# Two seams of an up projection in a decoder step: operands in a written order, sums moved between engines

## The chip, the cores and the metric

The kernel runs on one core of a Trainium2 chip. A core has five engines with queues of their own: TensorE (PE, matmuls; PEld is its weight load), VectorE (DVE), ScalarE (ACT), GpSimd (POOL) and SyncE (SP, which here only issues DMAs). Each works off its instructions in order and waits on semaphores. The metric is the device time of one execution in microseconds, lower is better.

## The reference

One step of a single-layer hybrid decoder for 1024 prompt rows and 64 sample rows of width 1024 (1088 rows, handled here as two halves of 544). What matters here is the end of it:

```python
merged = jax.nn.sigmoid(ga) * (o_a @ w_a_out[i]) + jax.nn.sigmoid(gb) * (o_b @ w_b_out[i])
x = x + merged @ w_o[i]
h2 = rmsnorm(x, g_mlp[i])
x = x + jnp.square(jax.nn.relu(h2 @ w_up[i])) @ w_down[i]
y = rmsnorm(x, g_final).astype(out_dtype)
```

w_o is 1024 x 1024, w_up 1024 x 4096, w_down 4096 x 1024, all in 32-bit floats.

## The kernel before

Every 32-bit product is made of three matmuls: each operand is split into a high part (a cast, on ScalarE) and a low part (operand minus high part, on VectorE; called a low below), and high x high, high x low and low x high are summed in PSUM (`mm3`, `product`). `split` is that pair of instructions; their rows are `z<-..., CAST` and `z<-...,z TENSOR_TENSOR`.

*Output projection.* `project(c)` makes x + merged @ w_o for half c of the rows in eight steps of 128 output features, 48 matmuls each, two halves, so 16 steps; steps 13, 14 and 15 in the text are the last three. A step loads its weights and its part of x, splits the weights (`weights`, wh and wl), and after the matmuls adds x on VectorE (`scalar_tensor_tensor`, L1132, PSUM to `tmp`), stores the sum (x1_d) by a GpSimd DMA, scales it into F on ScalarE (L1137), squares it (L1142), adds the squares on GpSimd (L1143), takes differences in F on VectorE (L1144) and splits seven such blocks into the operands of the up projection (`ops`, kept in `self.B`). `norm2` (L1161) makes 1 / rms of the rows out of the squares: in its first half twelve one-column matmuls (six cuts), then a reciprocal root of ten small VectorE rows (`rsqrt`, L91 to L96); in its second half six transposes and a copy to `rb`.

*Up projection.* It runs with Strassen's scheme in Winograd's form: two k halves, two column halves, seven products for each of 16 pairs of 128 columns. `a_raw` loads the weights of a pair (two `raw`, 512 KB each), `a_op(i, q)` makes operand q of pair i, with sums S on VectorE for q = 2 to 5. `up_pair` runs the seven products in banks b1, b2 and b3 of PSUM: each run q is 24 matmuls for both halves of the rows (12 for pair 0, which is done half by half: c=0, then c=1); between the runs it copies a bank (`copied`, L1245), adds (`plus`, L1264), takes relu and rb (`done`: scalar_tensor_tensor L1251, Square L1252), takes differences on GpSimd (`less`, L1260), and stores the results with DMAs of SyncE (`keep`, F_d). A run that goes on in bank b1 waits for the copy of what is in it.

*Down projection.* It runs in steps over groups of 512 inner rows (g), halves of the rows (c) and of the columns (pp), again with seven products in the order 0, 3, 2, 1, 4, 5, 6 (`down_step`). Its B operands come back from F_d (`db_load`, `db_op`), its A operands from w_down (`da_raw`, sums `da_sum` on GpSimd, `da_op`); `low` makes the low part of either. Results are added to x1: for products 0, 2 and 4 through a copy on ScalarE (L1471) and an add on GpSimd (L1475), for the others by an add on VectorE that reads PSUM.

*What sets the order.* Up to the end of `project` a scheduler of the framework orders the instructions. `up_all` and `down_all` stand in `manual_schedule`: there each engine's order is that of the code. What is made for later steps is put between the runs by `side(q)`, before or after the copies of a run (`before`, `after`), and, from pair 14, by events with a due time (`plan_down`, `events`; the last up run is at about -1, the first down product at 0, two units per run in the up projection). `slot` gives SBUF places by the time until which each is used. The first seam is the passage from output projection to pair 0, the second the passage from pair 15 to the first down step.

## Time and profile before

| | |
|---|---|
| runs | 1541.91, 1543.89, 8198.35 us (median 1543.89) |
| the profiled execution | 1539.15 us, span of its instructions 1536.7 us |
| TensorE busy | 97% of the span, 10,907 matmuls |
| VectorE, ScalarE, GpSimd busy | 72%, 40%, 26% |
| granted TensorE clock, mean | 0.993 of full speed |
| output projection, steps 14 and 15 | TensorE from 804.4 to 816.5 us |
| up projection | 816.5 to 1167.8 us |
| down projection | from 1167.8 us |

The page lists busy time by engine, the span in 40 slices, the chain of work that ended last, the costliest groups of instructions and the DMA issues. The trace behind it answers for a stretch: the instructions of an engine in order of time (start, duration, engine, line, operation, output<-inputs, shapes, count, and in brackets the idle time before with what ended it), who waited for whom, and busy time and granted clock in chosen stretches. In such rows successive alike instructions are merged, and buffer numbers are left out.

### The profile page before, as it was taken

Reading aid. Unit: us, or ns where it says so; the run is one execution under the profiler, and the core shown is the slowest. Engines: PE = TensorE matmul, PEld = TensorE weight load, DVE = VectorE, ACT = ScalarE, POOL = GpSimd, SP = SyncE. Lnnn points to the kernel's source line nnn. Section 1 sums busy time; section 2 is a strip of 40 time slices with the busy share of each in tenths; the row PEclk is TensorE's granted clock in tenths of the full one; section 3 lists DMA queues with packets and bytes.
Section 4 is the critical chain, followed back from the end, with each engine's and each line's share of the span. In section 5 each row is a group of like instructions: output and inputs, shape, how many; then the busy total and the mean of one; then the engine's idle time right before and its main releaser. Section 6 shows DMA issues by size and latency. Waiting matters only on the chain.

```text
span 1536.7 us, 28328 instructions
## 1 busy us (share of the span) xinstructions
PE 1485.0 (97%) x10907; PEld 1446.0 (94%) x10907; DVE 1102.4 (72%) x2192; ACT 609.6 (40%) x1299; POOL 405.2 (26%) x336
## 2 busy tenths in 40 slices
PE   6999999999999999999999999999998999999996
PEld 5889999998998999999998999999997999999996
DVE  8686867757746256555878676666667999999985
ACT  5342332423413224222654443434435445445444
POOL 3200000000001012100332233222345666555641
PEclk9999999999999999999999999999999999999999
DMA  6432331332232434444553443344447544454423
GB/s 219 150 99 53 100 91 49 110 96 73 65 100 68 133 92 131 144 135 123 182 160 128 135 155 132 130 141 155 153 152 264 189 148 126 147 158 137 150 65 117
DMA packets 192367, 198.01 MB, mean 129 GB/s; under 512 B 22036, under 2 KB 157693, under 8 KB 192225
## 3 DMA queue, kind: packets, MB, share of 16 engines
q1 hardware_dynamic: 186953, 183.98, 38.2%
q0 software_dynamic: 4080, 12.13, 2.4%
q8 instruction: 85, 1.39, 0.4%
q14 instruction: 49, 0.40, 0.1%
q10 hardware_dynamic: 1200, 0.10, 0.1%
HBM read 132.10 MB, written 64.19 MB: 128 GB/s over the span
## 4 chain that ended last, share of the span: by engine, by line
PE 86%; DVE 6%; DMA 4%; ACT 2%; issue 1%; SPq 0%; DVEq 0%; ACTq 0%
PE pp L1228 21%; PE pp L1465 21%; PE pm L147 10%; PE pm L148 10%; PE pm L149 10%; PE pt L728 2%; PE pp L147 2%; PE pp L149 2%; PE pp L148 2%; DMA qk<-g_d 2%; PE pt L84 1%; DMA z<-F_d 1%; PE pp L84 1%; DVE r L108 1%; PE pc L817 1%
## 5 line engine op out<-in xcount | busy, mean ns | idle before, releaser
L1228 PE MATMUL pp<-z,z 128*128 128x272 f32 x2688 | 342.0, 290 | 7.5 <-ACT tmp L1245 4.9
L1228 PEld LDWEIGHTS pp<-z,z 128*128 128x128 f32 x2688 | 340.6, 190 | 8.4 <-ACT tmp L1245 5.3
L1465 PE MATMUL pp<-z,z 128*128 128x272 f32 x2688 | 343.0, 289 | 3.6 <-ACT tmp L1471 3.0
L1465 PEld LDWEIGHTS pp<-z,z 128*128 128x128 f32 x2688 | 339.2, 189 | 4.3 <-ACT tmp L1471 3.2
L147 PE MATMUL pm<-hi,wh 128*128 128x384 f32 (+1 forms) x840 | 283.6, 338 | 0.1
L148 PE MATMUL pm<-lo,wh 128*128 128x384 f32 (+1 forms) x840 | 281.6, 335 | 1.3 <-DVE lo L423 1.3
L149 PE MATMUL pm<-hi,wl 128*128 128x384 f32 (+1 forms) x840 | 279.7, 333 | 0.0
L148 PEld LDWEIGHTS pm<-lo,wh 128*128 128x128 f32 x840 | 159.1, 189 | 3.5 <-DVE lo L423 1.8
L147 PEld LDWEIGHTS pm<-hi,wh 128*128 128x128 f32 x840 | 158.9, 189 | 2.5 <-DVE hi L419 0.5
L149 PEld LDWEIGHTS pm<-hi,wl 128*128 128x128 f32 x840 | 159.0, 189 | 0.2
L1475 POOL TENSOR_TENSOR z<-z,tmp 128x544 f32<-128x544 f32 x75 | 110.5, 1473 | 136.6 <-ACT tmp L1471 136.6
L1451 DVE TENSOR_TENSOR z<-z 128x544 fp32r<-128x544 f32 x112 | 136.6, 1231 | 5.0 <-ACT z L1446 5.0
L136 DVE TENSOR_TENSOR wl<-wr,wh 128x1024 fp32r<-128x1024 f32 x57 | 69.8, 1224 | 55.6 <-ACT wh L135 49.0
L135 ACT CAST wh<-wr 128x1024 fp32r<-128x1024 f32 x57 | 59.8, 1049 | 122.5 <-PE pm L148 74.8
L1471 ACT COPY tmp<-pp 128x544 f32<-128x544 f32 x75 | 46.0, 614 | 151.8 <-PE pp L1465 151.8
L1044 DVE TENSOR_TENSOR z<-raw,z 128x512 fp32r<-128x512 f32 x48 | 65.2, 1382 | 36.8 <-ACT z L1043 36.7
L1475 DVE TENSOR_TENSOR z<-z,pp 128x544 f32<-128x544 f32 (+1 forms) x101 | 71.3, 706 | 26.7 <-PE pp L1465 25.1
L1260 POOL TENSOR_TENSOR tmp<-tmp,tq 128x544 f32<-128x544 f32 (+1 forms) x17 | 21.9, 1288 | 238.9 <-ACT tmp L1252 238.9
L1446 ACT CAST z<-z 128x544 fp32r<-128x544 f32 x112 | 70.4, 648 | 12.0 <-DMA z<-F_d 11.9
L149 PE MATMUL pp<-z,wl 128*128 128x272 f32 x256 | 74.1, 289 | 0.0
L147 PE MATMUL pp<-z,wh 128*128 128x272 f32 x256 | 73.9, 289 | 0.0
L148 PE MATMUL pp<-z,wh 128*128 128x272 f32 x256 | 73.6, 288 | 0.0
(344 smaller groups left out, 2510.9 us busy)
## 6 DMA issues: line engine op xcount, KB each, us to landing
z<-F_d SPq DMA_DIRECT2D x112, 272.0 KB
wr<-in_w_in_dram SPq DMA_DIRECT2D x33, 512.0 KB
raw<-in_w_up_dram SPq DMA_DIRECT2D x32, 512.0 KB
raw<-in_w_down_dram SPq DMA_DIRECT2D x32, 512.0 KB
F_d<-tmp SPq DMA_DIRECT2D x60, 272.0 KB
wr<-in_w_o_dram SPq DMA_DIRECT2D x16, 512.0 KB
F_d<-t SPq DMA_DIRECT2D x30, 272.0 KB
tmp<-xT_d SPq DMA_DIRECT2D x16, 272.0 KB
```

The lines of the kernel that those rows point to most:

```text
L135: nc.scalar.copy(out=hi, in_=raw)
L136: (nc.gpsimd if early else nc.vector).tensor_tensor(out=lo, in0=raw, in1=hi.bitcast(F32), op=ALU.subtract)
L147: mm(ps, lhsT=wh, rhs=xh, start=first, stop=False)
L148: mm(ps, lhsT=wh, rhs=xl, start=False, stop=False)
L149: mm(ps, lhsT=wl, rhs=xh, start=False, stop=last)
L1044: (eng or self.nc.vector).tensor_tensor(out=lo, in0=f, in1=hi.bitcast(F32), op=ALU.subtract)
L1228: mm(out, lhsT=l[:, k, :], rhs=r[:, k, :], start=first and k + n == 0, stop=k == 3 and n == 2, skip_group_check=not first)
L1446: self.nc.scalar.copy(out=hi, in_=lo.bitcast(F32))
L1451: self.nc.vector.tensor_tensor(out=lo, in0=f, in1=hi.bitcast(F32), op=ALU.subtract)
L1465: nc.tensor.matmul(ps[:, p, 0:CB], lhsT=l[:, k, p, :], rhs=r[:, k, :], start=first and j + k + n == 0, stop=j == len(gs) - 1 and k == 1 an ...
L1471: nc.scalar.copy(out=t, in_=ps[:, :, 0:CB])
L1475: eng.tensor_tensor(out=x, in0=x, in1=t, op=ALU.add)
```

## The change

1. `project` is taken apart into `fetch`, `parts`, `project`, `x1`, `b_op`; steps 13 to 15 (`project_end`) now stand in the written order. Step 15's addition of x comes inside pair 0's first half (after run 0), and its seven operands are spread over the runs there and one run of the second half. Pair 0's first three operands and its sums S are made behind step 14, the sums in place in `raw`.
2. `norm2` cuts the 544 rows into five pieces instead of six; its second half for c=1 is called at run 6 of pair 0's first half instead of run 5.
3. Operands of pair 1 are made one run later or more, those of pair 2 in the last four runs of pair 1, two at a time. Pairs 1 and 15 put `side` behind the copies of a run; pairs 2 to 14 ahead of them, as before.
4. Sums of the first w_down group (g = 0) on VectorE, at written times from -24 on; loads of the first w_down operand at -28, at the end of pair 13; due times of the first A operands spread. The differences of pair 15 (`less`) on VectorE.
5. The first down step adds all products on VectorE out of PSUM (`direct`), and its `side` comes behind the add.
6. Three more places X, and a smaller scratch for DMA descriptors (`dynamic_dma_scratch_size=4096`).

```diff
+                for n in (13, 14):
+                    self.fetch(n)
+                self.parts(13)
                 with tc.manual_schedule():
+                    self.project_end()
                     self.up_all()
...
+    def project_end(self):
+        for n in (13, 14, 15):
+            self.project(n)
+            if n < 15:
+                self.parts(n + 1)
+            if n == 13:
+                self.fetch(15)
+            elif n == 14:
                 self.a_raw(0)
+            else:
+                self.a_op(0, 0)
+                self.a_op(0, 1)
+                self.a_sum0(0)
+                self.a_op(0, 2)
+            if n < 15:
+                self.after(n)
...
-        cuts = [(b, j, min(P, CB - j * P)) for b in range(2) for j in range(3)]
+        cuts = [(n, n * P, min(P, CT - n * P)) for n in range(5)]
...
-            nc.gpsimd.tensor_tensor(out=at(o), in0=at(a), in1=at(b), op=ALU.subtract)
+            (v if i == 15 else nc.gpsimd).tensor_tensor(out=at(o), in0=at(a), in1=at(b), op=ALU.subtract)
...
         def first(q):
             self.t += 1
             if q == 0:
+                self.a_sum0(1)
                 self.a_raw(1)
-            if q < 3:
-                self.a_op(0, q + 4)
-            if q in (3, 5):
-                self.norm2(1, self.acc1, q == 5)
+            if q < 4:
+                self.a_op(0, q + 3)
+            if q >= 3:
+                b_op((1, 2, 4, 5)[q - 3])
+            if q in (3, 6):
+                self.norm2(1, self.accs[1], q == 6)
         def second(q):
             self.t += 1
             if q == 0:
+                b_op(6)
                 self.a_raw(2)
-            self.a_op(1, q)
+            if q >= 3:
+                self.a_op(1, q - 3)
...
-        self.up_pair(0, (0,), first, True)
-        self.up_pair(0, (1,), second)
+        self.up_pair(0, (0,), lambda q: q or self.x1(15), first)
+        self.up_pair(0, (1,), nothing, second)
+        ops = {(i, q): [(i + 1, q)] for i in range(1, 16) for q in range(7)}
+        ops.update({(1, q): [[(1, 4)], [(1, 5)], [(1, 6)], [(2, 0), (2, 1)], [(2, 2), (2, 3)], [(2, 4), (2, 5)], [(2, 6)]][q]
+                    for q in range(7)})
...
-            self.up_pair(i, (0, 1), side)
+            self.up_pair(i, (0, 1), *((side, nothing) if 1 < i < 15 else (nothing, side)))
...
-                u = 2 * u - 5 if (g, n) == (0, 0) else u
+                z = (-22, -9, -11, -18, -7, -5, -3)[q] if (g, n) == (0, 0) else u - 6
                 if q == 0:
-                    at(u - 20, self.da_raw, g, n)
+                    at(-28 if (g, n) == (0, 0) else u - 20, self.da_raw, g, n)
                 if 2 <= q < 6:
-                    at(max(u - 10, -14), self.da_sum, g, n, q)
+                    j = (3, 2, 4, 5).index(q)
+                    at(u - 10 if g else ((-24, -22, -20, -9), (-6, -4, -2, 5))[n][j], self.da_sum, g, n, q)
...
-        po = self.nc.gpsimd
+        po = self.nc.gpsimd if g else self.nc.vector
...
-                add(x, copied(b), po)
+                if direct:
+                    add(x, b[:, :, 0:CB], v)
+                else:
+                    add(x, copied(b), po)
...
-            self.down_step(gs, c, pp, b, side, left <= 3, left == 1)
+            self.down_step(gs, c, pp, b, side, left <= 3 or n == 0, left == 1, n == 0)
```

The rows below are the engines' instructions in order, the numbers behind the names are those of buffers. First VectorE at the end of the first half of pair 0, from the last row of the reciprocal root (rs<-rt,rs) to the scalar_tensor_tensor that empties bank b1 (tmp<-pp), before the change:

```order
L96 SCALAR_TENSOR_TENSOR rs_1589_9242<-rt_1590_9243,rs_1589_9242 128x6
L1264 TENSOR_TENSOR tmp_1586_9225<-tmp_1586_9225,tmp_1591_9266 128x272
L1251 SCALAR_TENSOR_TENSOR tmp_1586_9225<-tmp_1586_9225,rb_7907 128x272
L1264 TENSOR_TENSOR tmp_1584_9208<-tmp_1584_9208,pp_1577_9152 128x272
L1251 SCALAR_TENSOR_TENSOR tmp_1584_9208<-tmp_1584_9208,rb_7907 128x272
L1251 SCALAR_TENSOR_TENSOR tmp_1595_9315<-pp_1575_9150,rb_7907 128x272
```

and after it:

```order
L96 SCALAR_TENSOR_TENSOR rs_1588_9222<-rt_1589_9223,rs_1588_9222 128x6
L1313 TENSOR_TENSOR tmp_1584_9205<-tmp_1584_9205,tmp_1590_9246 128x272
L1300 SCALAR_TENSOR_TENSOR tmp_1584_9205<-tmp_1584_9205,rb_7907 128x272
L1054 TENSOR_TENSOR z_1507_8563<-F_1566_9051,z_1506_8562 128x272
L1313 TENSOR_TENSOR tmp_1582_9188<-tmp_1582_9188,pp_1575_9125 128x272
L1300 SCALAR_TENSOR_TENSOR tmp_1582_9188<-tmp_1582_9188,rb_7907 128x272
L1054 TENSOR_TENSOR z_1511_8567<-F_1566_9051,z_1510_8566 128x272
L1300 SCALAR_TENSOR_TENSOR tmp_1593_9291<-pp_1573_9123,rb_7907 128x272
```

The two lows of step 15's operands, z<-F,z, stand now between the root and that last row.

Next VectorE in pair 14, around the plus on tq (tq<-tq,pp) behind run 1, before the change (S and z<-raw,z belong to pair 15):

```order
L1044 TENSOR_TENSOR z_1879_12540<-raw_1859_12306,z_1879_12540 128x512
L1044 TENSOR_TENSOR z_1881_12569<-raw_1860_12307,z_1881_12569 128x512
L1264 TENSOR_TENSOR tq_1880_12543<-tq_1880_12543,pp_1877_12514 128x544
L1251 SCALAR_TENSOR_TENSOR tq_1880_12543<-tq_1880_12543,rb_7907 128x544
L1209 TENSOR_TENSOR S_1882_12600<-raw_1859_12306,raw_1860_12307 128x512
L1210 TENSOR_TENSOR S_1882_12600<-S_1882_12600,raw_1859_12306 128x512
L1044 TENSOR_TENSOR z_1883_12603<-S_1882_12600,z_1883_12603 128x512
L1044 TENSOR_TENSOR z_1885_12632<-S_1882_12600,z_1885_12632 128x512
```

and after it (raw_1874 and raw_1875 are the halves of w_down's first operand, z_1883 is the place of their sums):

```order
L1054 TENSOR_TENSOR z_1880_12531<-raw_1858_12293,z_1880_12531 128x512
L1054 TENSOR_TENSOR z_1882_12560<-raw_1859_12294,z_1882_12560 128x512
L1480 TENSOR_TENSOR z_1883_12563<-raw_1874_12494,raw_1875_12495 128x512
L1313 TENSOR_TENSOR tq_1881_12534<-tq_1881_12534,pp_1878_12505 128x544
L1300 SCALAR_TENSOR_TENSOR tq_1881_12534<-tq_1881_12534,rb_7907 128x544
L1243 TENSOR_TENSOR S_1884_12593<-raw_1858_12293,raw_1859_12294 128x512
L1244 TENSOR_TENSOR S_1884_12593<-S_1884_12593,raw_1858_12293 128x512
L1054 TENSOR_TENSOR z_1885_12596<-S_1884_12593,z_1885_12596 128x512
L1482 TENSOR_TENSOR z_1883_12563<-z_1883_12563,raw_1874_12494 128x512
L1054 TENSOR_TENSOR z_1888_12628<-S_1884_12593,z_1888_12628 128x512
L1513 TENSOR_TENSOR z_1886_12599<-raw_1874_12494,z_1886_12599 128x512
```

The first sum of w_down's operand stands now ahead of the plus on tq.

Last VectorE from the second plus of pair 15 (tmp<-tmp,pp) to the first add of the down projection, before the change (L1475, z<-z,pp; the add of product 0 was GpSimd's, so this one is product 3's):

```order
L1264 TENSOR_TENSOR tmp_1913_12864<-tmp_1913_12864,pp_1898_12749 128x544
L1251 SCALAR_TENSOR_TENSOR tmp_1913_12864<-tmp_1913_12864,rb_7907 128x544
L1451 TENSOR_TENSOR z_1924_13006<-S_1900_12776,z_1924_13006 128x512
L1251 SCALAR_TENSOR_TENSOR tmp_1927_13016<-pp_1896_12747,rb_7907 128x544
L1451 TENSOR_TENSOR z_1931_13037<-raw_1887_12636,z_1931_13037 128x512
L1451 TENSOR_TENSOR z_1932_13039<-raw_1901_12778,z_1932_13039 128x512
L1475 TENSOR_TENSOR z_1912_12861<-z_1912_12861,pp_1930_13024 128x2x272
```

and after it (L1309 is `less`, L1537 the add, here of product 0):

```order
L1309 TENSOR_TENSOR tmp_1917_12908<-tmp_1909_12840,tq_1901_12771 128x544
L1309 TENSOR_TENSOR tmp_1909_12840<-tmp_1913_12874,tmp_1909_12840 128x544
L1309 TENSOR_TENSOR t24_1921_12955<-tmp_1913_12874,tmp_1917_12908 128x544
L1513 TENSOR_TENSOR z_1907_12811<-z_1907_12811 128x544
L1513 TENSOR_TENSOR z_1908_12814<-z_1908_12814 128x544
L1513 TENSOR_TENSOR z_1923_12965<-raw_1875_12495,z_1923_12965 128x512
L1484 TENSOR_TENSOR raw_1903_12775<-raw_1903_12775 128x4x128
L1300 SCALAR_TENSOR_TENSOR tmp_1924_12995<-pp_1898_12744,rb_7907 128x544
L1309 TENSOR_TENSOR t24_1922_12956<-tmp_1924_12995,t24_1921_12955 128x544
L1513 TENSOR_TENSOR z_1911_12844<-z_1911_12844 128x544
L1513 TENSOR_TENSOR z_1912_12848<-z_1912_12848 128x544
L1537 TENSOR_TENSOR z_1919_12922<-z_1919_12922,pp_1927_13011 128x2x272
```

The differences of pair 15 and a sum of w_down stand now ahead of the first add, which reads the bank itself.

## Rows read from the trace of the kernel before

**Rows 1.** The page: busy time of the engines; the chain that ended last, by engine.

```profile
PE 1485.0 (97%) x10907; PEld 1446.0 (94%) x10907; DVE 1102.4 (72%) x2192; ACT 609.6 (40%) x1299; POOL 405.2 (26%) x336
...
PE 86%; DVE 6%; DMA 4%; ACT 2%; issue 1%; SPq 0%; DVEq 0%; ACTq 0%
```

**Rows 2.** TensorE's waits from 795 to 1200 us: total, times, longest.

```profile
PE pp L1228 <- ACT tmp L1245: 4.9, 2, 4.4
```

**Rows 3.** Timeline of TensorE, 812 to 840 us: start, duration, instructions, idle before.

```profile
822.51 4.80 PE L1228 MATMUL pp<-z,z 128*128 128x272 f32 x24 [2.66 <-ACT tq L1245]
827.15 1.30 PE L1169 MATMUL pp<-one,acc 128*128 128x1 f32 x12
...
831.49 1.05 PE L84 MATMUL pp<-ident,rs 128*128 128x128 f32 x6
832.48 7.78 PE L1228 MATMUL pp<-z,z 128*128 128x272 f32 x60
```

**Rows 4.** The same view, 1147 to 1197 us.

```profile
1157.10 10.82 PE L1228 MATMUL pp<-z,z 128*128 128x272 f32 x72 [4.40 <-ACT tmp L1245]
...
1173.91 21.55 PE L1465 MATMUL pp<-z,z 128*128 128x272 f32 x156 [2.98 <-ACT tmp L1471]
1196.09 1.15 PE L1465 MATMUL pp<-z,z 128*128 128x272 f32 x7 [0.63 <-DVE z L1475]
```

**Rows 5.** Stretches of 10 us: length, TensorE busy (matmuls), granted clock, DMA share, GB/s.

```profile
820.00:830.00 10.00, 7.49 (x49) 0.83 0.12 43
...
840.00:850.00 10.00, 9.51 (x76) 1.00 0.35 122
850.00:860.00 10.00, 10.00 (x82) 1.00 0.60 194
...
1170.00:1180.00 10.00, 7.02 (x44) 0.83 0.69 234
```

**Rows 6.** Timeline of VectorE, 812 to 840 us.

```profile
819.43 2.29 DVE L1144 TENSOR_TENSOR F<-F 128x272 f32<-128x272 f32 x3 [0.22 <-ACT F L1137]
```

**Rows 7.** Timeline of VectorE and ScalarE, 830 to 835 us.

```profile
830.81 0.17 DVE L96 SCALAR_TENSOR_TENSOR rs<-rt,rs 128x6 f32<-128x6 f32 x1
830.92 0.44 DVE L1264 TENSOR_TENSOR tmp<-tmp,tmp 128x272 f32<-128x272 f32 x1
...
831.87 0.43 ACT L1252 ACTIVATE tmp<-tmp 128x272 f32<-128x272 f32 x1 [1.29 <-DVE tmp L1251]
```

**Rows 8.** Timeline of VectorE and ScalarE, 1126 to 1132 us.

```profile
1126.61 0.71 DVE L1264 TENSOR_TENSOR tq<-tq,pp 128x544 f32<-128x544 f32 x1
...
1130.02 0.60 ACT L1245 COPY tmp<-pp 128x544 f32<-128x544 f32 x1
...
1131.79 0.62 ACT L1245 COPY tmp<-pp 128x544 f32<-128x544 f32 x1 [0.65 <-PE pp L1228]
```

**Rows 9.** Timeline of SyncE's issues, 1104 to 1108 and 1119 to 1136 us.

```profile
1105.48 0.99 SPq L1190 DMA_DIRECT2D raw<-in_w_up_dram  x2
...
1124.39 0.32 SPq L1257 DMA_DIRECT2D F_d<-t  x1
```

**Rows 10.** DMA, 1100 to 1112 us: what was moved, in 40 slices.

```profile
GB/s 0 0 0 189 348 370 22 0 0 210 384 326 7 73 370 392 370 428 225 138 305 370 208 130 154 290 345 369 376 365 382 358 376 394 442 290 58 7 7 15
```

**Rows 11.** The chain that ended last, 1145 to 1176 us: start, duration, what.

```profile
1150.18 6.40 DMA z<-F_d
```

**Rows 12.** Timeline of ScalarE, 1147 to 1197 us.

```profile
1155.15 1.38 ACT L1446 CAST z<-z 128x544 fp32r<-128x544 f32 x2 [2.81 <-DMA z<-F_d]
```

**Rows 13.** Timeline of VectorE, 1147 to 1197 us.

```profile
1158.20 2.44 DVE L1451 TENSOR_TENSOR z<-z 128x544 fp32r<-128x544 f32 x2
...
1164.27 0.73 DVE L1251 SCALAR_TENSOR_TENSOR tmp<-tmp,rb 128x544 f32<-128x544 f32 x1
1164.91 0.72 DVE L1451 TENSOR_TENSOR z<-z 128x544 fp32r<-128x544 f32 x1
...
1166.84 0.71 DVE L1264 TENSOR_TENSOR tmp<-tmp,pp 128x544 f32<-128x544 f32 x1
```

More of the change, by code (lines that the diff above doesn't have):

```diff
@@ L268, in build @@
             self.X = right("Z", ctx)
[L269 removed]
+            self.places = ([(-300, ("Y", n)) for n in (16, 17)] + [(-290, ("X", n)) for n in range(21)]
                            + [(-270 + n // 8, ("Y", n)) for n in range(16)])
@@ new lines, in fetch, with parts, project @@
+    def fetch(self, n):
+        c, m = n // KD, n % KD // 2 + 4 * (n % 2)
+        self.pws[n] = self.load(self.a["w_o"][0, :, m * P:(m + 1) * P], KD)
+        self.pxs[n] = self.tmp()
+        self.nc.sync.dma_start(out=self.pxs[n], in_=self.xT_d[m, :, c * CT:(c + 1) * CT])
+    def parts(self, n):
+        self.pws[n] = self.weights(None, KD, raw=self.pws[n])
+    def project(self, n):
+        w, c = self.pws.pop(n), n // KD
+        ps = self.pps = self.ppn()
+        for b in range(2):
+            for k in range(KD):
+                xh, xl = (t[:, k % 2, b * CB:(b + 1) * CB] for t in self.mg[c][k // 2])
+                self.mm3(ps[:, b, 0:CB], w[0][:, k, :], w[1][:, k, :], xh, xl, k == 0, k == KD - 1)
@@ L1175, in norm2 @@
             return
-        ps = self.pp()
-        for n, (b, j, rows) in enumerate(cuts):
-            self.tr(ps[:, b, j * P:j * P + rows], self.rstd2[0:rows, n:n + 1].broadcast_to([rows, P]), rows)
-        nc.scalar.copy(out=self.halves(self.rb[:, c * CT:(c + 1) * CT]), in_=ps[:, :, 0:CB])
+        ps = self.pp().rearrange("p b t -> p (b t)")
+        for n, at, rows in cuts:
+            self.tr(ps[:, at:at + rows], self.rstd2[0:rows, n:n + 1].broadcast_to([rows, P]), rows)
+        nc.scalar.copy(out=self.rb[:, c * CT:(c + 1) * CT], in_=ps[:, 0:CT])
     def a_raw(self, i):
@@ L1219, in a_op, with a_sum0 @@
         self.aops[i, q] = hi, lo
+    def a_sum0(self, part):
+        v = self.nc.vector
+        r0, r1 = self.raws[0]
+        half = lambda t, n: t[:, :, n * P:(n + 1) * P]
+        if part == 0:
+            t = self.wp.tile([P, D], F32, name=self.name("S"), tag="wh", bufs=2)
+            S = self.ss_[0] = [t[:, n * 512:(n + 1) * 512].rearrange("p (k c) -> p k c", k=4) for n in range(2)] + [half(r0, 1)]
+            v.tensor_tensor(out=S[0], in0=half(r0, 1), in1=half(r1, 1), op=ALU.add)
+            v.tensor_tensor(out=S[1], in0=S[0], in1=half(r0, 0), op=ALU.subtract)
+            v.tensor_tensor(out=S[2], in0=half(r0, 0), in1=S[2], op=ALU.subtract)
+        else:
+            S = self.ss_[0]
+            v.tensor_tensor(out=S[1], in0=half(r1, 0), in1=S[1], op=ALU.subtract)
     def product(self, i, q, ps, c, first):
@@ L1229, in product, with up_pair @@
                    skip_group_check=not first)
-    def up_pair(self, i, cs, side, late=False):
+    def up_pair(self, i, cs, before, after):
         nc, v = self.nc, self.nc.vector
@@ L1264, in plus @@
             v.tensor_tensor(out=at(t), in0=at(t), in1=ps, op=ALU.add)
-        before = (lambda q: None) if late else side
-        after = side if late else (lambda q: None)
         run(0, b1, True)
@@ L1451, in low, with down_step @@
         self.nc.vector.tensor_tensor(out=lo, in0=f, in1=hi.bitcast(F32), op=ALU.subtract)
-    def down_step(self, gs, c, pp, banks, side, first, last):
+    def down_step(self, gs, c, pp, banks, side, first, last, direct=False):
         nc, v, po = self.nc, self.nc.vector, self.nc.gpsimd
```

156 lines of the change are left out of this document (74 added, 82 removed).

## The prediction

> **What bounds the kernel now.** The page comes first: TensorE is busy 97% of the span and holds 86% of the chain that ended last [rows 1]. A change that leaves the matmuls of the projections as they are can only move time in which TensorE stands still or runs below its full clock. The second view is TensorE's waits between 795 and 1200 us: it waits for ScalarE's copies of finished banks; the largest line has 4.9 us in two waits, one of 4.4 [rows 2]. The third, TensorE's timeline, gives the places: 2.66 us up to 822.51 in the first up pair (the first seam) [rows 3], 4.40 up to 1157.10 in the last up pair and 2.98 up to 1173.91 in the first down step (the second seam), and 0.63 for a VectorE add in the next [rows 4]; the other wait of the 4.9 is 0.5 us, in 840 to 850. The fourth is the table of 10 us stretches [rows 5]: one at full speed holds 82 matmuls. Two with long stalls have a granted clock of 0.83, that with the 0.5 us stall 1.00. So the clock fell from its 2.4 GHz level to its 1.2 GHz level behind the long stalls, and not behind the short one. What a fall costs: 1170 to 1180 has 44 matmuls, 38 fewer than 82; at 10 / 82 = 0.122 us each that is 4.64 us, of which 2.98 are the stall. I use the remaining 1.65.
>
> The most that the change could win is 2.66 + 0.49 + 4.40 + 2.98 + 0.63 = 11.2 us of stalls and 3 x 1.65 = 4.95 of clock: 16.1 us, 1% of the span. About 2% (31 us) is what a measurement of this kernel tells from no change.
>
> **The change part by part.** All times are those of the profiled execution (1539.15 us, span 1536.7).
>
> *The second norm, five cuts for six.* Two of twelve one-column matmuls go (1.30 / 12 x 2 = 0.2 us) and one of six transposes (1.05 / 6 = 0.17) [rows 3]. For the first half of the columns this lies on TensorE's path: -0.4. For the second half VectorE decides, next.
>
> *First seam.* In the kernel before, the copy that ends the 2.66 us stall stands on ScalarE behind a cast that waits for VectorE's three subtractions at 819.43, which take 2.29 us [rows 6]. The new order spreads those casts over the later runs. There are waits still: pair 0's operands and three sums now stand ahead of step 15's scalar_tensor_tensor, which comes some 1.6 us later. But I count short stalls (0.8, 1.4 and 0.9 us), which keep the clock, and TensorE comes to the second half of pair 0 some 1.6 us earlier, at about 832.4. There the new wait is. VectorE's order shows that the last scalar_tensor_tensor of the first half (tmp<-pp, which frees the bank that the second half's first run needs) now has two lows (z<-F,z) more between it and the reciprocal root; that run's bank was another one before, freed by the copy of rb. Each low waits for a cast that stands behind a Square on ScalarE. From the root's last row, which ends at 831.0 [rows 7] and by my count at 831.2 after: plus and scalar_tensor_tensor 0.9, then Square, cast and low at 0.43 each (the Square's row) 1.3, the next two 0.9, the next three 1.3, the last 0.44: 836.05, and 0.2 for a low beside a GpSimd difference. Before, that run began when the first 12 of the 60 matmuls from 832.48 were through (12 / 60 of 7.78), at about 834.05 [rows 3]. So +2.2, and a stall of 3.8 us, with a fall of the clock, as behind the long ones: +1.65. The short stall after 840 goes, -0.5. Together +3.3 (bounds: +0.1 if VectorE uses all of TensorE's lead of 1.6 and the clock stays; +4.1 if every low runs beside GpSimd).
>
> *Pairs 1 and 2.* Pair 2's operands are crowded into pair 1's last runs, two at a time. In the steady pairs the copy that run 4 needs is ready 0.9 us ahead: in pair 14 it ends at 1130.62, and run 4 follows run 3, whose bank is copied from 1131.79, so at about 1131.5 [rows 8]. By my count pair 2 enters 1.7 us late: +0.9 (0 to +1.7).
>
> *Pair 14.* The sums of the first down step come to VectorE. The first (z<-raw,raw) stands now ahead of plus tq, where VectorE arrives at 1126.61 [rows 8]. Its operands are two loads of w_down, 512 KB each, which SyncE issues behind the store F_d<-t of 1124.39 [rows 9], the second at about 1125.3. Of the pair of loads before it the second was issued in 1105.48 to 1106.47, near 1106.0 [rows 9], and the DMA engines carry them until about 1111.0 (in the row's slices of 0.3 us the rate falls from 290 over 58 to 7 GB/s there) [rows 10]: 5.0 us. So the sum starts at about 1130.2, 3.6 us after VectorE is free, and plus tq follows at 1130.9. In the kernel before the copy for run 4 ends 4.0 us after plus tq begins (1126.61 to 1130.62), with the same two sums and the cast between: so at 1134.9, or 1135.3 with what ScalarE now has ahead of it. Run 4 starts 3.8 us late, and the clock falls: +5.4. If the loads take a fifth less, 1.0 of it goes; if 6.4 us, as the F_d load on the chain [rows 11], it is +6.9.
>
> The Trainium skill ("DMA: Bandwidth & Descriptors", Anatomy of one DMA) gives about 2.0 us plus bytes over 436 GB/s, for a DMA issued by GpSimd; an estimate by that for 1 MB from the first issue is 4.4 us, so 1129.2 in place of 1130.2, and the term would be 1.0 us smaller. The row is slower than the page, and I keep to the row.
>
> *Pair 15.* Copies go first, so the copy behind the 4.40 us, which stood behind casts that waited 2.81 us for an F_d load [rows 12], is ready before run 4. The stall and its fall of the clock go, and TensorE would reach the third product of the first down step at 1173.91 - 2.98 - 4.40 - 1.65 = 1164.9.
>
> *First down step, direct.* Its adds read PSUM on VectorE. The third product needs the first add, which is queued behind all that VectorE has left. The copy after run 4 ends at about 1156.4 in the new time (1157.10 - 4.40 = 1152.7 for run 4's start, 24 x 0.122 = 2.9 for its matmuls, 0.8 until the copy is through); from there to the first add the order has 19 rows: two plus, three scalar_tensor_tensors, four differences that GpSimd did before, eight lows, two sums. Rows of 128 x 544 follow one another every 0.65 us [rows 13]: 12.4 us; two waits for a Square add 0.7 each, the add itself 0.71 [rows 13]. That is 1170.9. So the 2.98 us stall becomes one of 6.0 with the same fall of the clock, and the product starts 3.0 us earlier than at 1173.91: -3.0 for the whole seam (bounds: -10.7 if VectorE has no backlog, 9.0 us of start and one fall; -0.7 if the rows take 0.77 each). The 0.63 us should go with GpSimd's adds: -0.5.
>
> Sum: -0.4 + 3.3 + 0.9 + 5.4 - 3.0 - 0.5 = +5.7 us; 1544.9 on the profiled execution. The two ordinary runs shown, 1541.91 and 1543.89, lie 2.8 and 4.7 above it; I add the smaller: 1547.6, and say 1547.
>
> **The rivals.** Times are worked out as there, from 1541.9.
> *VectorE has no backlog* (faster; one mechanism at both seams). Beside GpSimd's sums VectorE's rows are long: two lows took 2.44 us at 1158.20, against 0.72 for one alone [rows 13]. Those neighbours go. If VectorE gets through its rows before TensorE asks, the first seam gives -2.66 - 0.49 - 1.65 = -4.8, the second -10.7; with -0.4, -0.5 and pair 14's +5.4 that is -11.0: 1531. It decides where the 19 rows and the add end by 1164.9, 6 us before my count; against it speaks that 19 x 0.65 alone is 12.4 us. Chance 0.2. The Trainium skill ("SBUF — State Buffer", Who interferes with whom) has the rule: a VectorE instruction with two SBUF inputs and a GpSimd instruction that reads SBUF share an interface, which the first holds while the second waits. The row of 2.44 us agrees.
> *The loads are there in time.* If the w_down loads land by 1127.6, run 4 of pair 14 doesn't wait, and 5.7 - 5.4 = +0.3: 1542. Against it: the second issue alone is at 1125.3. Chance 0.15.
> *All at the upper bounds:* -0.4 + 4.1 + 1.7 + 6.9 - 0.7 = +11.6: 1553.5. Chance 0.1.
> *Everything closes,* pair 14 too: -16.1 - 0.4: 1525. Chance 0.1.
>
> **How the numbers follow.** My forecast has 0.45, with a range of its own of 1543 to 1552. The range of 1531 to 1555 reaches to the second case on either side and leaves out the last rival and some accident. All cases lie inside 2%: faster 0.01, same 0.98, slower 0.01.
>
> **What would show it.** Right: among TensorE's waits one of 3 to 4 us in pair 14, ended by a copy whose chain goes back to a load of w_down; one of 3 to 4 us at the second half of pair 0, ended by a scalar_tensor_tensor; one of about 6 us at the third down product, ended by a VectorE add; no wait at run 4 of pair 15; and clocks under 0.9 in the 10 us behind each of the three. Wrong: no such wait in pair 14, or the third down product within 1 us of the second.

## The result and the profile after

The changed kernel takes 1558.86 us in the median of five runs (1550.92 to 1560.55), the kernel before 1542.27 in the median of its five (four from 1539.27 to 1543.89 and one of 8198.35, which the ratio leaves out): 0.97% slower, ratio 1.0097 with a 95% interval of 1.0079 to 1.0116. The forecast had the direction and put the time at 1547, with a range that ended at 1555; the median lies 11.9 us above the one and 3.9 above the other.

The profiled execution of the changed kernel is the fastest of the five, 1550.92 us (span 1548.8), 11.8 us over that of the kernel before (1539.15). Counting the matmuls of each product line in the trace gives the time at which each pair and each down step begins; the differences of these times add up to the span. "Before" and "after" are one profile each:

| stretch of TensorE's work, us | before | after | difference | forecast |
|---|---|---|---|---|
| up to the first matmul of pair 0 | 816.50 | 816.32 | -0.18 | -0.4 |
| pair 0 | 28.89 | 31.78 | +2.89 | +3.3 |
| pairs 1 and 2 | 42.15 | 48.78 | +6.63 | +0.9 |
| pairs 3 to 13 | 231.88 | 231.66 | -0.22 | 0 |
| pair 14 | 21.08 | 28.41 | +7.33 | +5.4 |
| pair 15 and the first down step | 42.56 | 40.39 | -2.17 | -3.0 |
| second and third down step | 22.15 | 21.07 | -1.08 | -0.5 |
| the rest | 331.52 | 330.37 | -1.15 | 0 |
| span | 1536.73 | 1548.79 | +12.06 | +5.7 |

The page's lines that answer to [rows 1], of the changed kernel:

```profile
PE 1486.9 (96%) x10901; PEld 1448.1 (94%) x10901; DVE 1103.1 (71%) x2199; ACT 606.6 (39%) x1296; POOL 378.0 (24%) x321
...
PE 83%; DVE 7%; DMA 5%; ACT 3%; issue 2%; SPq 0%; ACTq 0%; DVEq 0%
```

TensorE is as busy as before in microseconds (1486.9 against 1485.0), but its part of the chain falls from 86 to 83%; GpSimd has lost 27 us of work and VectorE's total has hardly moved. So the 12 us are not more work. TensorE's waits from 790 to 1220 us, the view of [rows 2]:

```profile
PE pp L1527 <- DVE z L1537: 7.2, 1, 7.2
PE pp L1277 <- ACT tq L1294: 6.5, 3, 4.0
PE pp L1277 <- ACT tmp L1294: 4.9, 1, 4.9
PE pp L1277 <- DVE tmp L1300: 3.1, 1, 3.1
PE pp L149 <- DVE wl L136: 0.6, 1, 0.6
PE pp L1277 <- DVE z L1054: 0.4, 1, 0.4
```

They add up to 22.7 us (the 0.6 for `wl` lies ahead of pair 0), where the five waits of the kernel before (2.66, 0.49, 4.40, 2.98 and 0.63) had 11.2. TensorE's timeline gives their places, as [rows 3, 4] do for the kernel before; in this excerpt the second half of pair 0 starts at 835.93, run 2 of pair 2 at 880.21, run 4 of pair 14 at 1145.65, the third down product at 1188.41:

```profile
821.37 2.38 PE L1277 MATMUL pp<-z,z 128*128 128x272 f32 x14 [1.86 <-ACT tq L1294]
...
835.93 18.35 PE L1277 MATMUL pp<-z,z 128*128 128x272 f32 x132 [3.10 <-DVE tmp L1300]
854.87 21.33 PE L1277 MATMUL pp<-z,z 128*128 128x272 f32 x168 [0.59 <-ACT tq L1294]
880.21 10.06 PE L1277 MATMUL pp<-z,z 128*128 128x272 f32 x66 [4.01 <-ACT tq L1294]
...
1145.65 32.52 PE L1277 MATMUL pp<-z,z 128*128 128x272 f32 x240 [4.91 <-ACT tmp L1294]
1188.41 11.85 PE L1527 MATMUL pp<-z,z 128*128 128x272 f32 x82 [7.25 <-DVE z L1537]
```

The waits of the kernel before at run 4 of pair 15 (4.40) and in the second down step (0.63) are gone; the one at the third down product (2.98) is 7.25. Stretches of 10 us with a granted clock under 1, the view of [rows 5]:

```profile
820.00:830.00 10.00, 8.27 (x54) 0.83 0.11 42
830.00:840.00 10.00, 6.89 (x43) 0.83 0.22 73
...
880.00:890.00 10.00, 9.79 (x66) 0.83 0.52 169
...
1140.00:1150.00 10.00, 5.09 (x25) 0.68 0.20 75
1150.00:1160.00 10.00, 10.00 (x80) 0.98 0.08 30
...
1180.00:1190.00 10.00, 2.75 (x17) 0.73 0.65 227
```

There are five falls to the 1.2 GHz level instead of three. At the wait of pair 14, 1140 to 1160 lacks 59 matmuls of 164, 7.2 us at 0.122; less the 4.91 that is 2.3 us for the fall, where 1.65 was taken.

**Why pair 2 waits.** Timeline of VectorE, ScalarE and GpSimd around the end of pair 1 (L1309 are GpSimd's differences, L1248 a sum for pair 2's operand 5, L1300 the scalar_tensor_tensor that empties pair 1's last bank, L1301 its Square, L1294 the copy that run 2 of pair 2 waits for):

```profile
871.85 1.36 POOL L1309 TENSOR_TENSOR tmp<-tmp,tq 128x544 f32<-128x544 f32 x1 [17.16 <-ACT tmp L1301]
872.37 1.40 DVE L1054 TENSOR_TENSOR z<-S,z 128x512 fp32r<-128x512 f32 x1 [0.69 <-ACT z L1053]
...
873.69 1.85 DVE L1248 TENSOR_TENSOR S<-raw,S 128x512 f32<-128x512 f32 x1
...
877.22 0.71 DVE L1300 SCALAR_TENSOR_TENSOR tmp<-pp,rb 128x544 f32<-128x544 f32 x1
877.97 0.66 ACT L1301 ACTIVATE tmp<-tmp 128x544 f32<-128x544 f32 x1 [1.72 <-DVE tmp L1300]
878.53 1.12 ACT L1053 CAST z<-raw 128x512 fp32r<-128x512 f32 x2
...
879.56 0.60 ACT L1294 COPY tq<-pp 128x544 f32<-128x544 f32 x1
```

Pair 1's last run ends at 870.0. Two operands of pair 2 (sum, cast and low each) are queued behind run 5, beside GpSimd, where a row of 0.69 us takes 1.40 or 1.85; so the row that empties the last bank comes at 877.22, 7.2 us behind the run. Its Square stands ahead of the copy on ScalarE, with two casts between, and run 2 begins when the copy is through, at 880.21. That copy isn't the one the prediction looked at. The same three rows (scalar_tensor_tensor, Square, copy) in the kernel before, where pair 1 ends at 866.5:

```profile
868.78 0.71 DVE L1251 SCALAR_TENSOR_TENSOR tmp<-pp,rb 128x544 f32<-128x544 f32 x1
...
869.52 0.66 ACT L1252 ACTIVATE tmp<-tmp 128x544 f32<-128x544 f32 x1 [2.14 <-DVE tmp L1251]
...
870.60 0.60 ACT L1245 COPY tq<-pp 128x544 f32<-128x544 f32 x1
```

There the row comes 2.3 us behind the run, and the copy is through at 871.2, 1.3 us before run 2 begins (872.5).

**Pair 14** is as forecast, only longer. SyncE's issue of the two loads, the sum that waits, the plus on tq behind it, and the copy that run 4 needs:

```profile
1133.95 2.30 SPq L1460 DMA_DIRECT2D raw<-in_w_down_dram  x2
...
1140.51 0.69 DVE L1480 TENSOR_TENSOR z<-raw,raw 128x512 f32<-128x512 f32 x1 [4.68 <-DMA raw<-in_w_down_dram]
1141.11 0.71 DVE L1313 TENSOR_TENSOR tq<-tq,pp 128x544 f32<-128x544 f32 x1
...
1144.99 0.60 ACT L1294 COPY tmp<-pp 128x544 f32<-128x544 f32 x1
```

VectorE stood for 4.68 us on a DMA, and counted from the pair's start this sum comes 1.2 us later than forecast; [rows 8] is the same place without it.

### The profile page after: what moved, and what is told of

The parts are those of the page before. It is cut to its first block, busy times and chain, and to the rows that moved or that the text cites. A ratio compares the mean times of both kernels' runs of the same rounds, so it can differ in the third digit from the quotient of the medians.

```text
span 1548.8 us, 28195 instructions
## 1 busy us (share of the span) xinstructions
PE 1486.9 (96%) x10901; PEld 1448.1 (94%) x10901; DVE 1103.1 (71%) x2199; ACT 606.6 (39%) x1296; POOL 378.0 (24%) x321
## 4 chain that ended last, share of the span: by engine, by line
PE 83%; DVE 7%; DMA 5%; ACT 3%; issue 2%; SPq 0%; ACTq 0%; DVEq 0%
PE pp L1527 21%; PE pp L1277 18%; PE pm L147 10%; PE pm L148 10%; PE pm L149 10%; PE pp L149 2%; PE pp L147 2%; PE pp L148 2%; PE pt L738 2%; DMA qk<-g_d 2%; PE pt L84 1%; ACT z L1053 1%; DVE r L108 1%; PE pp L84 1%; PE pc L827 1%
## 5 line engine op out<-in xcount | busy, mean ns | idle before, releaser
L1537 POOL TENSOR_TENSOR z<-z,tmp 128x544 f32<-128x544 f32 x72 | 102.3, 1420 | 172.6 <-ACT tmp L1533 172.6
L1513 DVE TENSOR_TENSOR z<-z 128x544 fp32r<-128x544 f32 x112 | 132.5, 1195 | 0.6 <-ACT z L1508 0.6
L1537 DVE TENSOR_TENSOR z<-z,pp 128x544 f32<-128x544 f32 (+1 forms) x104 | 73.6, 708 | 29.7 <-PE pp L1527 28.5
L1309 POOL TENSOR_TENSOR tmp<-tmp,tq 128x544 f32<-128x544 f32 (+1 forms) x16 | 20.6, 1285 | 244.2 <-ACT tmp L1301 244.2
L1054 DVE TENSOR_TENSOR z<-S,z 128x512 fp32r<-128x512 f32 x63 | 45.3, 720 | 37.6 <-ACT z L1053 37.4
```

The costliest lines, as they stand in the source:

```text
L1054: (eng or self.nc.vector).tensor_tensor(out=lo, in0=f, in1=hi.bitcast(F32), op=ALU.subtract)
L1513: self.nc.vector.tensor_tensor(out=lo, in0=f, in1=hi.bitcast(F32), op=ALU.subtract)
L1537: eng.tensor_tensor(out=x, in0=x, in1=t, op=ALU.add)
```

## Experiments

Theory A in what follows: the loss is a sum of separate waits, each behind a queue on VectorE or ScalarE that one part of the change lengthens, with a fall of the clock behind the long ones. Times of stretches are those of one profile of each version.

**The changed kernel again.** No edit.

> The changed kernel once more. Theory A (waits): the same five places stand out among TensorE's waits as in its first profile (run 2 and the second half of pair 0, run 2 of pair 2, run 4 of pair 14, the third down product), and the spread of its runs (1551 to 1561 us) comes from how long these waits are and whether the clock falls behind them. Theory B (something spread over the program, such as GpSimd's DMAs with the smaller descriptor scratch): a slower execution is slower in stretches away from the seams, so that the steady pairs 3 to 13 take more than 231.7 us.

Measured: 1556.69 us (four runs, 1551.38 to 1562.78), ratio 1.0096 (1.0061 to 1.0131). Its profile has the same waits: 1.60, 3.94, 4.01, 5.84 and 7.54 us. Pairs 3 to 13 take 231.66 us in both profiles, so the steady part is the same to the digit. The span is 7.8 us longer than in the first profile: 5.1 of it lies ahead of pair 0 (821.42 us against 816.32), 0.7 in pair 14, 1.6 in pair 15 and the first down step. The time up to pair 0 lies between 816.3 and 824.3 us in the fourteen profiles of this study, also in the three that have the code of the kernel before up to there (816.50, 817.92 and 821.80). So theory A is right about the places and wrong about the spread: most of it isn't made at the seams. Theory B finds support only ahead of pair 0, and the smaller scratch isn't needed for that: 816.50 and 821.80 are both with the old one.

**First seam alone.**

```diff
-            (v if i == 15 else nc.gpsimd).tensor_tensor(...)
+            nc.gpsimd.tensor_tensor(...)
-                if i == 13 and q == 6:
+                if i == 14 and q == 3:
                     self.plan_down()
...
-            self.up_pair(i, (0, 1), *((side, nothing) if 1 < i < 15 else (nothing, side)))
+            self.up_pair(i, (0, 1), *((side, nothing) if 1 < i else (nothing, side)))
```

plan_down, da_sum and down_all as in the kernel before; the three places and the smaller scratch stay.

> First seam, crowding of pair 2 and the new norm alone; pair 14 on, sums, differences and first down step as in the kernel before. Theory A: TensorE reaches pair 3 9.3 us later than in the kernel before, as in the changed kernel, then the old waits of 4.4 and 3.0 us stay: +9 us, about 1551. Theory C (the two seams hang together, the late start of pair 3 costs nothing by itself): under +4 us. Theory B (descriptor scratch): over +10 us, with runs spread over 10 us.

Measured: 1549.85 us, ratio 1.0064 (1.0040 to 1.0088), +8 us by the medians and +10 by the ratio. Pair 0 takes 31.44 us and pairs 1 and 2 48.83: +9.2 over the kernel before, as expected by theory A. Pair 15 and the first step take 41.39 us (42.56 before).

**Second seam alone.** The parts just taken out, put into the kernel before (with three more places and the smaller scratch).

> Second seam alone, on the kernel before. Theory A: +7.3 us at pair 15 from the wait of 4.9 us in pair 14 and its clock fall, -2.2 up to the second down step, -1.2 behind it: +4 us, about 1546. Theory C: no loss, 0 or less. Theory B: over +10 us, with runs spread over 10 us.

Measured: 1546.73 us, ratio 1.0027 (1.0014 to 1.0041), +5.1 us by the medians and +4.2 by the ratio. Pair 14 takes 28.55 us (+7.5), pair 15 and the first step 40.34 (-2.2), the two next steps 21.07 (-1.1). The two seams add up (0.64 + 0.27 = 0.91%, against 0.97 for both): theory C falls, and for the scratch as a large cost of its own nothing is left.

The next five versions ran once each (1549.94, 1550.39, 1552.95, 1555.63 and 1561.71 us in this order). With several us of spread ahead of pair 0, single times decide nothing between them; they are read by their stretches.

**Later sums in pair 14.**

```diff
-                z = (-22, -9, -11, -18, -7, -5, -3)[q] if (g, n) == (0, 0) else u - 6
+                z = (-20, -9, -11, -18, -7, -5, -3)[q] if (g, n) == (0, 0) else u - 6
-                    ... ((-24, -22, -20, -9), (-6, -4, -2, 5))[n][j], self.da_sum, g, n, q)
+                    ... ((-20, -18, -16, -9), (-6, -4, -2, 5))[n][j], self.da_sum, g, n, q)
```

> The changed kernel with the first three sums of w_down and the first cast due at -20, -18, -16 and -20 in place of -24, -22, -20 and -22. Theory A: VectorE meets them some 4 us later, behind the landing of the loads, the wait of 4.9 us at run 4 of pair 14 and its clock fall go, TensorE starts pair 15 7.3 us earlier relative to pair 14 (21.1 us after it, as in the kernel before). Rival: the wait isn't the loads' but VectorE's load of work, and only moves to run 5 or 6 or to pair 15: pair 15 still starts over 25 us after pair 14.

Measured: pair 14 takes 21.06 us, and TensorE waits nowhere in it. Of its VectorE timeline, the sums of S now follow the plus on tq, and the first sum of w_down comes after:

```profile
1139.31 0.71 DVE L1313 TENSOR_TENSOR tq<-tq,pp 128x544 f32<-128x544 f32 x1
...
1145.07 0.69 DVE L1480 TENSOR_TENSOR z<-raw,raw 128x512 f32<-128x512 f32 x1 [0.55 <-DMA raw<-in_w_down_dram]
```

It still waits 0.55 us for the load, but nothing that TensorE needs is behind it in time. The 7.3 us of pair 14 are shown to be the sums' wait for those loads. Not all of it is won: the wait at the third down product grew to 8.31, and pair 15 and the first step take 43.25 us, 2.9 more than in the changed kernel. From the start of pair 0 to the fourth down step 8.4 us of loss remain, against 13.4.

**Late operands of step 15 in the second half of pair 0.**

```diff
-            if q >= 3:
-                b_op((1, 2, 4, 5)[q - 3])
+            if q == 3:
+                b_op(1)
...
+            if q < 4:
+                b_op((2, 4, 5, 6)[q])
             if q == 0:
-                b_op(6)
                 self.a_raw(2)
```

> The changed kernel with four of the five late operands of step 15 (products 2, 4, 5, 6) made in the second half of pair 0, runs 0 to 3, instead of the first. Theory A (the lows in front of the last scalar_tensor_tensor hold the bank): the wait of 2.4 to 3.9 us at the second half's first run falls below 1 us and its clock fall goes; from the start of pair 0 to that of pair 1 27.4 to 28.8 us, against 31.8 in the changed kernel and 28.9 in the kernel before. Rival: the operands, now later, are waited for in the second half, and it stays at 30 us or more.

Measured: the wait is 1.09 us (below 1 was expected) and the clock is 1.00 in 820 to 850; pair 0 takes 27.07 us, 1.8 less than in the kernel before. Theory A holds: two lows in a queue cost the first seam its gain. Pairs 1 and 2 take 49.64, not better: theirs is another wait.

**Pair 2's operands a run earlier.**

```diff
-[[(1, 4)], [(1, 5)], [(1, 6)], [(2, 0), (2, 1)], [(2, 2), (2, 3)], [(2, 4), (2, 5)], [(2, 6)]]
+[[(1, 4)], [(1, 5)], [(1, 6), (2, 0)], [(2, 1), (2, 2)], [(2, 3), (2, 4)], [(2, 5)], [(2, 6)]]
```

> The changed kernel with the operands of pair 2 made one run earlier each: pairs of them behind runs 2, 3 and 4 of pair 1 and one behind 5. Theory A (two operands behind run 5 hold up the last scalar_tensor_tensor of pair 1, and so the Square, the casts and the copy that run 2 of pair 2 needs): the wait of 4.0 us shrinks by 2 to 3.5 us, the clock stays, pair 2 takes 21.1 to 23.5 us instead of 26.9 (5.8 over the kernel before). Rival (GpSimd's differences beside it slow VectorE, whatever the operands): over 25 us.

Measured: pairs 1 and 2 take 45.72 us, 3.1 less than in the changed kernel; the wait is 1.97 us and the clock in 880 to 890 is 1.00. Pair 2 takes 23.80 us, just over the range of theory A. One operand behind run 5 instead of two halves the wait: the crowding, not GpSimd alone. The other half stays, so GpSimd's share isn't excluded.

**Copies and GpSimd's adds in the first down step.**

```diff
-            self.down_step(gs, c, pp, b, side, left <= 3 or n == 0, left == 1, n == 0)
+            self.down_step(gs, c, pp, b, side, left <= 3 or n == 0, left == 1)
```

> The changed kernel with the copies on ScalarE and the adds on GpSimd again in the first down step. Theory A (the wait of 7.3 us at the third down product is VectorE's load of work, not the way of the add): the copy stands on ScalarE behind the Square of pair 15's last bank, which waits for the same VectorE queue, so the wait shrinks by only 1 to 3 us. Rival (the direct add is the cause): it shrinks to under 2 us; from the first to the second down step 15.3 us as in the kernel before, instead of 19.3.

Measured: the wait is 6.09 us and ends with ScalarE's copy; first to second down step 18.7 us (19.3 in the changed kernel). The way of the add is not the cause.

**Differences of pair 15 on GpSimd.**

```diff
-            (v if i == 15 else nc.gpsimd).tensor_tensor(...)
+            nc.gpsimd.tensor_tensor(...)
```

> The changed kernel with the four differences of pair 15 on GpSimd again. Theory A: three of them and two waits for Squares go from VectorE's queue ahead of the first down add, so the wait of 7.3 us falls to 3 to 5 us. Rival (VectorE is held there by loads or casts): no change within 1 us.

Measured: 8.14 us, longer than 7.25. VectorE and GpSimd in that stretch of this kernel:

```profile
1187.12 1.37 POOL L1309 TENSOR_TENSOR tmp<-tmp,tq 128x544 f32<-128x544 f32 x1 [15.79 <-ACT tmp L1301]
...
1187.61 1.46 DVE L1513 TENSOR_TENSOR z<-z 128x544 fp32r<-128x544 f32 x1 [0.62 <-ACT z L1508]
...
1189.00 1.81 DVE L1513 TENSOR_TENSOR z<-raw,z 128x512 fp32r<-128x512 f32 x1
1190.22 1.77 POOL L1309 TENSOR_TENSOR t<-tmp,tmp 128x544 f32<-128x544 f32 x1
1190.73 1.81 DVE L1484 TENSOR_TENSOR raw<-raw 128x512 f32<-128x512 f32 x1
...
1194.44 1.48 DVE L1513 TENSOR_TENSOR z<-z 128x544 fp32r<-128x544 f32 x1 [0.63 <-ACT z L1508]
```

Theory A's number was wrong here: four differences of 0.73 us leave VectorE's queue ahead of the first add (2.9 us, and two waits of 0.72 for Squares), but four rows that stay take 1.46, 1.81, 1.81 and 1.48 us beside GpSimd instead of about 0.7, 3.7 us more, and waits of 0.6 for casts come in. From the second plus's scalar_tensor_tensor to the first add VectorE needs 10.2 us instead of 9.3. In this one profile the differences on VectorE cost nothing.

**Only the copies first in pair 15**, on the kernel before.

```diff
-            self.up_pair(i, (0, 1), side)
+            self.up_pair(i, (0, 1), side, i == 15)
```

> The kernel before with one part of the change alone: in pair 15 the copies come ahead of the operands of later steps. Theory A (the 4.4 us wait of the kernel before is that order, and no other part of the change is needed against it): the 4.4 us wait and its clock fall go, 3 to 6 us faster, about 1537; some of it comes back if VectorE's adds for pair 15 are late. Rival (GpSimd's sums and the late F_d loads hold it anyway): the wait moves to run 5 or to the first down products, no gain over 1 us.

Measured: 1541.33 us, ratio 0.9996 (0.9979 to 1.0012), no difference. TensorE's waits in its timeline:

```profile
1163.25 6.30 PE L1228 MATMUL pp<-z,z 128*128 128x272 f32 x48 [2.15 <-ACT tmp L1245]
1177.62 11.68 PE L1465 MATMUL pp<-z,z 128*128 128x272 f32 x72 [5.02 <-ACT tmp L1471]
```

The 4.40 us at run 4 go, 2.15 come back at run 5 and 2.0 at the third down product. The rival holds: the order alone only moves the wait.

**Three new waits undone.** The edits of pair 14 and of the late operands above, and in place of the crowding a lag of three operands through pairs 1 to 6:

```diff
+        ops, n = {}, 11
+        for i in range(1, 16):
+            for q in range(7):
+                ops[i, q] = [divmod(n + k, 7) for k in range(2 if (i, q) in ((2, 4), (4, 4), (6, 4)) else 1)]
+                n += len(ops[i, q])
...
+            self.up_pair(i, (0, 1), *((side, nothing) if 6 < i < 15 else (nothing, side)))
```

> The changed kernel with the three new waits undone: sums of w_down four units later, late operands of step 15 in the second half, and pairs 1 to 6 three operands behind, one of which is caught up in each of pairs 2, 4 and 6, with the copies first there. Theory A adds up by places: start of pair 0 to pair 3 -1.8 + 0 to 1 us, pair 14 0, first down steps -0.4 to +0.7, behind them -1.2, all against the kernel before: between -4 and +1 us, about 1539. Rival (a load on VectorE that finds another place to wait): +4 us or more.

Measured: 1544.64 us, ratio 1.0022 (1.0004 to 1.0039). Pair 0 and pair 14 are right (27.29 and 21.06 us), but each operand caught up behind run 4 is followed by a wait at run 2 of the next pair (1.89, 0.56 and 1.09 us in pairs 3, 5 and 7): pairs 3 to 13 take 238.38 us, 6.5 more. It is the place at which pair 2 loses, three times over. At the second seam the third down product waits 8.17 us, and pair 15 and the first step take 42.87 us, 0.3 more than in the kernel before. The time lies between what theory A and the rival expected.

**The same first seam with the second seam of the kernel before.** The lag and the late operands on the kernel with the first seam alone, copies first in pair 15.

> The first seam of the changed kernel with its two new waits undone as in the kernel with three undone, and the second seam of the kernel before with the copies first in pair 15. Theory A: the sum of the two single gains, -1 to -2 us at the first seam and -3 to -6 at the second, so 4 to 8 us faster than the kernel before, about 1536. Rival: the second seam's gain was tied to where VectorE stood in the kernel before, and the sum stays above -2 us.

Measured: 1548.14 us, ratio 1.0036 (1.0022 to 1.0051). Slower, where 4 to 8 us faster was expected. Again pairs 3 to 13, 239.08 us; pair 15 and the first step take 41.22, 1.3 less than in the kernel before, so that the rival's low gain at the second seam came about too.

**No crowding at all.** Later sums in pair 14; four late operands behind runs 0 and 1 of the second half of pair 0, with all seven operands of pair 1 as in the kernel before; sums of the second w_down operand behind the first down products.

```diff
+            for k in ((2, 4), (5, 6))[q] if q < 2 else ():
+                b_op(k)
             if q == 0:
-                b_op(6)
                 self.a_raw(2)
-            if q >= 3:
-                self.a_op(1, q - 3)
+            self.a_op(1, q)
...
-        ops.update({(1, q): [[(1, 4)], [(1, 5)], [(1, 6)], ...
...
-                    ... ((-24, -22, -20, -9), (-6, -4, -2, 5))[n][j], self.da_sum, g, n, q)
+                    ... ((-20, -18, -16, -9), (1, 2, 4, 5))[n][j], self.da_sum, g, n, q)
```

> The changed kernel with its waits undone in another way: sums of w_down at -20, -18, -16; late operands of step 15 behind runs 0 and 1 of the second half of pair 0, together with all seven operands of pair 1, so that no later pair is crowded; the sums of the second w_down operand behind the first down products (1, 2, 4, 5) instead of -6 to 5. Theory A: start of pair 0 to pair 3 -1.8 to 0 us against the kernel before, pair 14 0, the wait at the third down product 1 to 2 us shorter than 8.2, all of the second seam and behind it -2 to -4: 2 to 5 us faster than the kernel before, about 1538. Rival: the second half of pair 0 can't hold all that VectorE work, pairs 1 to 3 lose 2 us or more, and it is no faster than the kernel before.

Measured: 1535.44 us against 1540.99, ratio 0.9962 (0.9949 to 0.9975): 0.4% faster than the kernel before, the only version that beats both. Its profile is the slowest of the six executions, 1541.05 us, with pair 0 starting at 822.96, 6.5 us later than in the kernel before's; so it is read from pair 0 on. Pair 0 takes 29.63 us, pairs 1 and 2 42.13, pair 14 21.06, pair 15 and the first down step 40.15, the next two 21.06. TensorE's longest waits from 790 to 1220 us:

```profile
PE pp L1525 <- DVE z L1535: 6.0, 1, 6.0
PE pp L1277 <- ACT tmp L1294: 2.0, 2, 1.1
PE pp L1277 <- ACT tq L1294: 2.0, 2, 1.6
PE pp L1277 <- DVE tmp L1300: 1.1, 1, 1.1
```

The second seam gives 2.4 us and the steps behind it 1.1, the first seam costs 0.7 in place of 1.8 gained, because pair 1's operands now crowd the second half (two waits of about 1 us there). The expected gain up to pair 3 failed by that, and the rival's loss stayed under 1 us. The third down product still waits 6 us.

## Why the prediction was right and wrong

*What failed.* Two steps, and the time left the range by both together; with either error alone it would have stayed inside. One is the term of pairs 1 and 2, +0.9 against +6.63. The other is the step from the profiled execution to an ordinary one, 2.8 us against 7.9.

*The bound.* Right: the change moved only TensorE's waits and its clock. Pairs 3 to 13 take 231.66 to 231.88 us in every profile of a kernel that keeps their order.

*Up to pair 0.* The term of -0.4 was near by luck. From TensorE's 5000th matmul (at about 761 us) to pair 0, profiles with the new code take 54.9 to 55.0 us and those with the old one 54.6: +0.3. The matmuls that go are outweighed by a wait of 0.57 us for `wl`, which the prediction didn't have; the -0.18 comes from ahead of the change.

*The second half of pair 0.* Right in place, mechanism and size: forecast a wait of 3.8 us with a fall of the clock and +3.3, found 3.10 and +2.89 (3.94 and +3.29 in the second profile). VectorE and ScalarE there, the rows that answer to [rows 7]:

```profile
830.83 0.17 DVE L96 SCALAR_TENSOR_TENSOR rs<-rt,rs 128x6 f32<-128x6 f32 x1
...
832.66 0.44 DVE L1054 TENSOR_TENSOR z<-F,z 128x272 fp32r<-128x272 f32 x1 [0.80 <-ACT z L1053]
...
834.73 0.79 DVE L1054 TENSOR_TENSOR z<-F,z 128x272 fp32r<-128x272 f32 x1 [0.80 <-ACT z L1053]
835.45 0.43 DVE L1300 SCALAR_TENSOR_TENSOR tmp<-pp,rb 128x272 f32<-128x272 f32 x1
```

The last row ends at 835.88, the count gave 836.25; the low at 834.73 does run beside a GpSimd row. Taking the lows away brought pair 0 to 27.07 us. One thing beside it was wrong: "short stalls ... which keep the clock". The stall of 1.86 us at run 2 was followed by 0.83 in 820 to 830. It decided nothing, since VectorE ends last here: in the second profile that stall was 1.60 us without a fall, and the second half started only 0.4 us earlier after the pair's start.

*Pairs 1 and 2.* This step failed, and it is most of the error of the sum: +6.63 against +0.9 (0 to +1.7). The prediction followed the copy that run 4 needs, since that was the one with 0.9 us of slack in [rows 8], and did not follow the copy of run 0, which run 2 needs and which had 1.3. That copy stands behind the Square of the pair before, whose input VectorE makes 7.2 us behind that pair's last run instead of 2.3. With 4.01 and 0.59 us of waits and a fall of the clock this term is 5.7 us too small. The move of one operand (45.72 us) and the version without crowding (42.13) show the crowding as its cause. The new order of copies and operands in pair 1 isn't: the version without crowding has it too.

*Pair 14.* Mechanism right, shown by the later sums (21.06 us). The size was off: +7.33 against +5.4. Two sizes in it were too small: the landing of the loads (a wait of 4.91 us where 3.8 was forecast) and the fall of the clock, 2.3 in place of 1.65. The sum's wait ended 6.0 us behind the second issue, where 5.0 was taken from one pair of loads [rows 9, 10]:

```profile
1134.45 1.80 SPq L1460 DMA_DIRECT2D raw<-in_w_down_dram  x1
```

Following the last semaphore update of each w_up load in the kernel before, the second of a pair landed 4.8 to 6.6 us behind its issue, from pair to pair. So the row taken was one of the quickest, and 6.0 us needs no other cause; what makes the difference isn't shown. The loads were not alone on SyncE either: it had F_d stores before and behind them in both kernels. The sentence on the Trainium skill ("DMA: Bandwidth & Descriptors", Anatomy of one DMA) pointed the wrong way, to 1.0 us less: 4.4 us from the first issue, where the trace has 6.5 (1133.95 to 1140.44).

*Second seam.* Right: the 4.40 us went, the third down product waits for a VectorE add behind that queue. Of VectorE's rows a wait for a cast, the second plus, the last scalar_tensor_tensor and the first add:

```profile
1175.64 0.72 DVE L1513 TENSOR_TENSOR z<-z 128x544 fp32r<-128x544 f32 x1 [0.62 <-ACT z L1508]
...
1177.49 0.72 DVE L1313 TENSOR_TENSOR tmp<-tmp,pp 128x544 f32<-128x544 f32 x1
...
1184.20 0.72 DVE L1300 SCALAR_TENSOR_TENSOR tmp<-pp,rb 128x544 f32<-128x544 f32 x1
...
1187.56 0.71 DVE L1537 TENSOR_TENSOR z<-z,pp 128x544 f32<-128x544 f32 x1
```

Forecast a stall of 6.0 us and -3.0, found 7.25 and -2.17. The 19 rows took 14.7 us (1172.90 to 1187.56) where the count had 13.8; 0.62 of it is the wait for a cast, which the count lacks. The first rival, no backlog on VectorE, is out: the wait was longer than in the forecast, not shorter. Its argument that VectorE gains where GpSimd's neighbours go was sound by itself: with the differences put back on GpSimd the wait grew to 8.14 us, from 7.25 and 7.54 in the two profiles of the changed kernel. The rule of the Trainium skill ("SBUF — State Buffer", Who interferes with whom) agrees with the rows of 1.46 to 1.81 us beside GpSimd there, against about 0.7 without it.

*Behind the seam.* -0.5 forecast; the next two steps gave -1.08 and the rest -1.15, which was not in the sum. The rest is in the tail, where three waits of 0.68, 0.86 and 0.86 us became two of 0.67 and 0.47; with the first seam alone, which has the three places and the smaller scratch too, the rest takes 330.30 us. Why was not tried.

*From the profile to the median.* The sum for the profiled execution missed by 6.4 us (+5.7 against +12.06 of span), which would have left the time at about 1553. The other 5 us or so of the miss come from the second step that failed: the prediction added 2.8 us to come from the profiled execution to an ordinary one, and the changed kernel's median lies 7.9 above its profile, the kernel before's 3.1. The profile of the changed kernel is the quickest of its nine executions. It started pair 0 at 816.32 us, in the other ten profiles with the same code up to there it is 818.9 to 824.3. That difference is there long before the first seam: TensorE's 2400th matmul starts at 363.64 us in this profile, at 366.0 to 369.7 in the ten. The old code with the old scratch has it as well (363.72 and 368.91). What makes it stays open.

*The limit of the measurement.* The prediction took 2% as what a measurement tells from no change; the interval of the result was 1.0079 to 1.0116, so the loss of 0.97% is clear.

## What to carry to other kernels

Where operands are moved out of a crowded place, list every bank copy and every row that frees a bank in the places they go to, with what is now ahead of each on its in-order engine, and not only the one with the least slack today. Do it for the whole queue across engines: the rows of an operand on VectorE held a Square, the Square held a copy, the copy held TensorE. A sum that needs a load belongs behind the rows that TensorE waits for until the load's landing is past, and a landing is better taken from many loads than from one; four time units (two runs of the up projection) were worth 7.3 us in pair 14, of which 2.9 came back at the third down product. And a profile is one execution: ask how far it lies from the median before its time is used as a base.
